# Attention on one core: TensorE's program regrouped, both heads' scores in one tile of three banks, value products' parts added on the way out of PSUM

## The chip, the cores and the metric

The kernel runs on one core of a Trainium2 chip. The metric is the device time of one execution in microseconds, as the median of several runs; less is better.

## What is computed

Two transformer blocks follow each other on 1024 tokens of width 1024, all in fp32. The change lies in the attention of the first. It has two kinds of head, eight each, of width 64: a windowed one (kind a: a block of 128 queries sees its own and the two neighbouring blocks of keys, 256 context keys and a sink) and a neighbourhood one (kind b: 128 queries see up to 384 keys with a bias, and 256 context keys).

```python
s_loc = einsum('bnqkgd,bnjkd->bnkgqj', qb, kb) * scale      # a; masked to the window
s_ctx = einsum('bnqkgd,bjkd->bnkgqj', qb, k_ctx) * scale
p = softmax(concatenate([s_loc, s_ctx, sink_col], axis=-1))
o_a = einsum(p_loc, vb) + einsum(p_ctx, v_ctx)
s_loc = einsum('bnqhd,bnjhd->bnhqj', qb, kg) * scale + bias # b; masked to the neighbourhood
p = softmax(concatenate([s_loc, s_ctx], axis=-1))
o_b = einsum(p_loc, vg) + einsum(p_ctx, v_ctx)
```

## The kernel before, in words

A fp32 factor of most products is cut into an upper part in the format fp32r and a lower part, the rest. The attention works on 64 units (`units`): 32 of kind a (block i, pair of heads p), then 32 of kind b (pair p, block i). A unit is two heads e = 0, 1 of one block of 128 queries, with three tiles of 128 local keys (two for i = 0 and 7) and two of context keys. Per unit these steps follow each other, each in a helper:

- `f_s` (L936): the scores of one head into PSUM, by the query's two parts: two products for the local keys (L948) and two for the context (L949). Each head has a tile `ps_s` of two banks, with two buffers. The order of local and context columns is chosen by `order` (L908) so that no product crosses a bank.
- `f_max` (L952): VectorE adds mask or bias, writes the negated scores to `sp` and reduces them to the softmax's shift (L961). It is the last reader of the score tile.
- `f_exp` (L966): ScalarE's exponential in place, with its sum (L971).
- `f_pt` (L974): the probabilities are transposed by TensorE (L241), four blocks of 128x128 to a bank, in groups 0, 1 and 2, into a PSUM tile `pp` (`pp_tile`, three buffers), and cut into the two parts in `pt`. For group 0 ScalarE copies the bank out (L993) and GpSimd makes both parts (L994, L995); for groups 1 and 2 ScalarE makes the upper part (L997) and VectorE the lower (L998).
- `f_pv` (L1000): the value products into the one bank of `ps_v`. For kind a (L1011) a block's two heads share a product, upper part and lower part in turn, accumulated in PSUM; for kind b (L1016) a product has one head's upper and lower part side by side, and their two results stay apart in PSUM. `part` is the half of the work (a) or the head (b). ScalarE copies the result out (L1022).
- `f_fin` (L1026): fp32 products with `twice` (L1035), a 128x64 matrix of two stacked identities, turn the result round and add what is still apart: one product per head for kind a, two for kind b. VectorE copies it to `O` (L1036).

The loop at L1179 runs software-pipelined: in step n, unit n gets its scores and reductions, unit n-1 the exponentials, unit n-2 the transposes, unit n-3 the value products, unit n-4 `f_fin`. Every second step turns a q tile (`conv_q`, L888, also a `pp` tile), whose reading also lets SP's queue issue the next q loads. Extra work is hung onto fixed steps: stacking kind b's keys (`b_k`: transposes on TensorE, copies on ScalarE, subtractions on VectorE), their values (`b_v`, GpSimd), the bias (`b_bias`: a product at L1106, sums on VectorE), normalizations (GpSimd L1050, L1057, L1069; a VectorE root at step 40, L248 to L261), and pieces of the next stage's weights (L142, L143). Each engine runs its instructions in the order in which this program issues them; a tile's buffer is given out again when all users of its last contents are done. In step n before, TensorE's order is: scores of head 0, group 0, scores of head 1, group 1, value products part 0, group 2, value products part 1, `f_fin`, q tile, extras.

Of the kernel before, what the change touches and what calls it, by code (L numbers as in the profile page):

```python
# [9 lines left out]
F32 = mybir.dt.float32  # L10
R32 = mybir.dt.float32r
I32 = mybir.dt.int32
AF = mybir.ActivationFunctionType
ALU = mybir.AluOpType
# [4 lines left out]
P = 128  # L19
D = 1024  # L20
KD = 8
S = 1024
# [190 lines left out]
def kernel(ctx: ExitStack, tc: tile.TileContext, a: dict, out: bass.AP, dbg=None):  # L213
    nc = tc.nc
# [25 lines left out]
    def tr(o, i, idn):  # L240
        nc.tensor.transpose(o, i, idn)  # L241
# [22 lines left out]
    ident = const.tile([P, P], F32, name="ident")  # L264
# [171 lines left out]
    for i in range(3):  # L436
        pt = ps_t.tile([P, 512], F32, tag="tp", name="vtp", bufs=2)
# [43 lines left out]
    for j in range(4):  # L481
        c = slice(j * 512, j * 512 + 512)
# [9 lines left out]
    for v in range(2):  # L492
        nc.vector.tensor_tensor(out=msum[:, v], in0=pmod[:, :, v], in1=bm, op=ALU.add)
        nc.vector.scalar_tensor_tensor(out=ab[:, v, 0], in0=msum[:, v, 8:16], scalar=1.0,
                                       in1=vec[:, voff["norm1"]:voff["norm1"] + 8], op0=ALU.add, op1=ALU.mult)
# [347 lines left out]
    zeros = zero1.broadcast_to([P, CTX])  # L843
    st_ps = ExitStack()
    ps_s = pool("ps_s", space=PSUM, stack=st_ps)
    ps_p = pool("ps_p", space=PSUM, stack=st_ps)
# [4 lines left out]
    maskA = wk.tile([P, 896], F32, name="maskA")  # L851
    twice = wk.tile([P, 64], F32, name="twice")
# [9 lines left out]
    A = {}  # L862

    def pp_tile():
        return ps_p.tile([P, 512], F32, tag="pp", name="pp", bufs=3)

    def stack_k(src, dst_a, dst_b, cols):

# [12 lines left out]
    def kt(i):  # L881
        return [j for j in (i - 1, i, i + 1) if 0 <= j < 8]
# [22 lines left out]
    def v_stack(u, e, tt):  # L905
        return VA[:, tt, u[2] // 2, :] if u[0] == "a" else B["v", u[2]][:, tt, e, :]

    def order(u, e):  # L908

        kk = kt(u[1])  # L910
        first = u[1] == 7 if u[0] == "a" else 0 < u[1] < 7 and e == 1
        return [8, 9] + kk if first else kk + [8, 9]

    def addends(u, e):

        i, p, nl = u[1], u[2], len(kt(u[1])) * P
        if u[0] == "a":
            a0 = 384 if i == 0 else 0 if i == 7 else 256
            return [(0, nl + 256, maskA[:, a0:a0 + nl + 256])]
        if i in (0, 7):  # L920
            ed = B["bE", p][:, e, (1 if i == 0 else 0):(3 if i == 0 else 2)].rearrange("p s r c -> p (s r c)")
            return [(0, nl, ed), (nl, 256, zeros)]
        return [(0, 640, B["bI", p][:, 0:640] if e == 0 else B["bI", p][:, 384:1024])]

    def stat(u):
# [8 lines left out]
    st = {}  # L934

    def f_s(x, e):  # L936
        u = units[x]
        kk = kt(u[1])
        nl = len(kk) * P
        c1 = order(u, e)[0] == 8  # L940
        w = nl + 256
        a0 = 512 - (256 if c1 else nl)
        ps = ps_s.tile([P, 1024], F32, tag="s", name="ps_s", bufs=2)[:, a0:a0 + w]
        lo, co = (256, 0) if c1 else (0, nl)
        k = k_stack(u, e)
        for z in range(2):
            q = qhl[x // 2][z][:, 2 * (x % 2) + e]
            nc.tensor.matmul(ps[:, lo:lo + nl], q, k[:, kk[0] * P:kk[0] * P + nl], start=(z == 0), stop=(z == 1))  # L948
            nc.tensor.matmul(ps[:, co:co + 256], q, k[:, 1024:1280], start=(z == 0), stop=(z == 1))  # L949
        st["s", x, e] = ps  # L950

    def f_max(x, e):  # L952

        u = units[x]
        if e == 0:
            st["sp", x] = wk.tile([P, 2, 640], F32, tag="sp", name="sp", bufs=3)
            st["nm", x] = stat(u)
        ps, nm = st.pop(("s", x, e)), st["nm", x][0][:, e:e + 1]
        at0 = nsink[:, 2 * u[2] + e:2 * u[2] + e + 1] if u[0] == "a" else -NEG
        for c0, n, in1 in addends(u, e):  # L960
            nc.vector.tensor_tensor_reduce(  # L961
                out=st["sp", x][:, e, c0:c0 + n], in0=ps[:, c0:c0 + n], in1=in1, scale=1.0, scalar=at0,
                op0=ALU.add, op1=ALU.min, accum_out=nm)
            at0 = nm

    def f_exp(x, e):  # L966
        u = units[x]
        nm, sm = st["nm", x]
        sp = st["sp", x]
        w = len(kt(u[1])) * P + 256  # L970
        nc.scalar.activation(out=sp[:, e, :w], in_=sp[:, e, :w], func=AF.Exp, bias=nm[:, e:e + 1], scale=-1.0,  # L971
                             accum_out=sm[:, e:e + 1])

    def f_pt(x, gi):  # L974
        u = units[x]
        nk = len(kt(u[1])) + 2
        if gi == 0:
            st["pt", x] = wk.tile([P, 10, 2, P], R32, tag="pt", name="pt", bufs=2)
        pt = st["pt", x]
        sp = st["sp", x] if gi < 2 else st.pop(("sp", x))  # L980
        g = list(range(4 * gi, min(4 * gi + 4, 2 * nk)))
        if not g:
            return
        pp = pp_tile()
        for x_, b in enumerate(g):
            j, e = b // 2, b % 2
            tr(pp[:, x_ * P:(x_ + 1) * P], sp[:, e, j * P:(j + 1) * P], ident)
        w = len(g) * P
        ph, pl = pt[:, g[0]:g[0] + len(g), 0, :], pt[:, g[0]:g[0] + len(g), 1, :]
        pv = pp[:, :w].rearrange("p (b t) -> p b t", t=P)  # L990
        if gi == 0:
            pf = wk.tile([P, 4, P], F32, tag="pf", name="pf", bufs=2)
            nc.scalar.activation(out=pf, in_=pv, func=AF.Copy)  # L993
            nc.gpsimd.tensor_copy(out=ph, in_=pf)  # L994
            nc.gpsimd.tensor_tensor(out=pl, in0=pf, in1=ph.bitcast(F32), op=ALU.subtract)  # L995
        else:
            nc.scalar.activation(out=ph, in_=pv, func=AF.Copy)  # L997
            nc.vector.tensor_tensor(out=pl, in0=pv, in1=ph.bitcast(F32), op=ALU.subtract)  # L998

    def f_pv(x, part):  # L1000
        u = units[x]
        tiles = [order(u, e) for e in range(2)]
        nt_ = len(tiles[0])
        pt = st["pt", x]
        if part == 0:
            st["po", x] = ps_v.tile([P, 512], F32, tag="pv", name="po")
        po = st["po", x]
        if u[0] == "a":
            for j in (range(nt_ - 2) if part == 0 else range(nt_ - 2, nt_)):
                for z in range(2):  # L1010
                    nc.tensor.matmul(po[:, 0:256], v_stack(u, 0, tiles[0][j]), pt[:, 2 * j:2 * j + 2, z, :],  # L1011
                                     start=(j == 0 and z == 0), stop=(j == nt_ - 1 and z == 1))
        else:
            e = part
            for j, tt in enumerate(tiles[e]):
                nc.tensor.matmul(po[:, e * 256:e * 256 + 256], v_stack(u, e, tt),  # L1016
                                 pt[:, 2 * j + e].rearrange("p z t -> p (z t)"),
                                 start=(j == 0), stop=(j == nt_ - 1))
        if part == 1:
            w = 256 if u[0] == "a" else 512  # L1020
            oT = wk.tile([P, 512], F32, tag="oT", name="oT", bufs=2)
            nc.scalar.activation(out=oT[:, :w], in_=po[:, :w], func=AF.Copy)  # L1022
            st["oT", x] = oT
            del st["pt", x], st["po", x]

    def f_fin(x):  # L1026

        kind, i, p = units[x]
        oT = st.pop(("oT", x))
        nb = 1 if kind == "a" else 2  # L1030
        po = pp_tile()
        for e in range(2):
            for j in range(nb):
                b = (nb * e + j) * P
                nc.tensor.matmul(po[:, e * 64:e * 64 + 64], oT[:, b:b + P], twice, start=(j == 0), stop=(j == nb - 1))  # L1035
        nc.vector.tensor_copy(out=O[0 if kind == "a" else 1][:, i, p * 128:p * 128 + 128], in_=po[:, 0:128])  # L1036


# [122 lines left out]
    for t in (maskB.rearrange("p r c -> p (r c)"), maskR, jrev):  # L1161
# [7 lines left out]
                            in0=maskP.rearrange("p (b c s) -> p b s c", s=8, c=8),  # L1169
# [6 lines left out]
    def ok(x):  # L1176
        return 0 <= x < NU

    for n in range(NU + 5):  # L1179
        if n == 35:  # L1180
            switch_pools()
        if ok(n):
            f_s(n, 0)
            f_max(n, 0)
        if ok(n - 1):
            f_exp(n - 1, 0)
        if ok(n - 2):
            f_pt(n - 2, 0)
        if ok(n):
            f_s(n, 1)  # L1190
            f_max(n, 1)
        if ok(n - 1):
            f_exp(n - 1, 1)
        if ok(n - 2):
            f_pt(n - 2, 1)
        if ok(n - 3):
            f_pv(n - 3, 0)
        if ok(n - 2):
            f_pt(n - 2, 2)
        if ok(n - 3):  # L1200
            f_pv(n - 3, 1)
        if ok(n - 4):
            f_fin(n - 4)
        if n % 2 == 0:
            conv_q(n // 2 + 1)
        for f, args in extra.get(n, []):
            f(*args)
# [242 lines left out]
    for i in range(8):  # L1450
        nc.gpsimd.tensor_tensor(out=O[1][:, i], in0=O[1][:, i],
                                in1=oss[:, 24 + i:25 + i].broadcast_to([P, 512]), op=ALU.mult)
    early = {}
    for n4 in range(2):
# [8 lines left out]
        for t in range(8):  # L1463
            ps = early.pop(t, None)
# [780 lines left out]
```

## Time and profile before

| | us |
|---|---|
| median of three runs | 2670.6 (2665.9 to 2671.87) |
| the profiled execution | 2668.49 |
| its span, from first to last instruction | 2666.7 |
| of it, TensorE busy | 2576.5 |
| VectorE, ScalarE, GpSimd busy | 1645.7, 1058.8, 1148.6 |

The attention's first score product starts at 312.73 us of the span, and its last product ends at about 624. The seven stretches below begin at the first score product of steps 0, 6, 18, 29, 36, 47 and 60. In the rows below PE is TensorE's product unit, PEld its weight loads, DVE is VectorE, ACT is ScalarE, POOL is GpSimd and SP is SyncE. A line such as L961 is one of the kernel's source lines; many rows of the trace stand on a helper's line, so tiles tell more than lines. The end of a TensorE row is modelled, and the rows of a stream overlap: their cost is the distance from start to start.

### The profile page before, as it was taken

The page shows a single profiled execution, that of the slowest core. Times are in us where ns is not written, and L with a number is a line of the kernel's source. Part 1 is how long each engine was busy: PE and PEld are TensorE (multiplying, and loading weights), DVE is VectorE, ACT ScalarE, POOL GpSimd, SP SyncE. Part 2 cuts the span into 40 slices and gives each one's busy share as a digit, 9 for nine tenths or more (in the row PEclk, how much of TensorE's full clock was granted, in tenths as well). Part 3 has the DMA queues.
Part 4 walks back from the last instruction along what each step waited for, and adds up shares of the span by engine and source line. Part 5 has one row for each costly group of instructions (what it writes and reads, how often), then busy time and mean ns, then how long its engine had stood idle before and what let it go on. Part 6 is the DMA issues. An engine that isn't in the chain of part 4 may idle for free. (4 is left out here: it accounts for less than half of the span.)

```text
span 2666.7 us, 37138 instructions
## 1 busy us (share of the span) xinstructions
PE 2576.5 (97%) x14053; PEld 2154.0 (81%) x14053; DVE 1645.7 (62%) x3003; ACT 1058.8 (40%) x2613; POOL 1148.6 (43%) x1071
## 2 busy tenths in 40 slices
PE   7999999999989999999999999999999999999998
PEld 3999898899977888888878877877777777777786
DVE  3688678774565555555556432422777777777776
ACT  4644488785232222222223534322433333333333
POOL 2355355564446666666653221212333333333321
PEclk9999999999999999999999999999999999999999
DMA  6166522212111111111111111110111111111112
GB/s 245 33 192 200 147 56 54 73 49 88 33 40 48 48 52 59 48 48 55 56 48 41 50 48 32 32 48 32 49 39 48 48 48 48 48 48 48 48 48 87
DMA packets 152540, 170.87 MB, mean 64 GB/s; under 512 B 39444, under 2 KB 135460, under 8 KB 151336
## 3 DMA queue, kind: packets, MB, share of 16 engines
q1 hardware_dynamic: 152200, 168.35, 19.9%
q8 instruction: 111, 1.82, 0.3%
q0 software_dynamic: 160, 0.14, 0.1%
q14 instruction: 69, 0.57, 0.1%
HBM read 154.81 MB, written 13.65 MB: 63 GB/s over the span
## 5 line engine op out<-in xcount | busy, mean ns | idle before, releaser
L140 POOL TENSOR_TENSOR wlo<-raw,whi 128x512 fp32r<-128x512 f32 x132 | 176.7, 1343 | 476.7 <-ACT whi L139 447.8
L1697 PE MATMUL pgu<-h,whi 128*128 128x512 f32 x864 | 342.4, 396 | 3.1 <-DVE h L1633 3.1
L1698 PE MATMUL pgu<-h,wlo 128*128 128x512 f32 x864 | 341.2, 395 | 0.5 <-POOL wlo L140 0.5
L1696 PE MATMUL pgu<-h,whi 128*128 128x512 f32 x864 | 341.4, 395 | 0.0
L140 DVE TENSOR_TENSOR wlo<-raw,whi 128x512 fp32r<-128x512 f32 (+2 forms) x304 | 221.3, 741 | 149.5 <-ACT whi L139 148.9
L139 ACT ACTIVATE whi<-raw 128x512 fp32r<-128x512 f32 (+1 forms) x436 | 232.2, 552 | 151.1 <-DMA raw<-in_w_down 61.0
L1715 DVE TENSOR_TENSOR uv<-pgu,uv 128x512 f32<-128x512 f32 x216 | 147.7, 687 | 150.0 <-PE pgu L1698 128.6
L237 PE MATMUL pdn<-wlo,hid 128*128 128x512 f32 x576 | 227.3, 395 | 4.5 <-DVE wlo L140 4.5
L236 PE MATMUL pdn<-whi,hid 128*128 128x512 f32 x576 | 226.4, 393 | 1.3 <-DVE uv L1410 1.0
L238 PE MATMUL pdn<-whi,hid 128*128 128x512 f32 x576 | 226.6, 393 | 0.0
L1411 POOL TENSOR_TENSOR x<-x,uv 128x512 f32<-128x512 f32 x144 | 192.2, 1355 | 31.6 <-DVE uv L1410 28.7
L1697 PEld LDWEIGHTS pgu<-h,whi 128*128 128x128 f32 x864 | 162.3, 188 | 42.3 <-DVE h L1633 3.6
L1696 PEld LDWEIGHTS pgu<-h,whi 128*128 128x128 f32 x864 | 162.5, 188 | 40.1
L1698 PEld LDWEIGHTS pgu<-h,wlo 128*128 128x128 f32 x864 | 162.1, 188 | 39.9 <-POOL wlo L140 0.9
L1718 POOL TENSOR_TENSOR uv<-uv 128x512 f32<-128x512 f32 x72 | 109.7, 1524 | 169.1 <-DVE uv L1715 169.1
L1566 POOL TENSOR_TENSOR hid<-sg,hid 128x512 fp32r<-128x512 f32 x80 | 118.0, 1479 | 132.0 <-ACT hid L1565 129.9
L236 PE MATMUL pin<-whi,h 128*128 128x256 f32 x512 | 146.8, 287 | 6.1 <-ACT hsq L634 2.5
L237 PE MATMUL pin<-wlo,h 128*128 128x256 f32 x512 | 146.7, 286 | 1.7 <-DVE wlo L140 1.7
L238 PE MATMUL pin<-whi,h 128*128 128x256 f32 x512 | 146.5, 286 | 0.0
L237 PEld LDWEIGHTS pdn<-wlo,hid 128*128 128x128 f32 x576 | 108.1, 188 | 34.1 <-DVE wlo L140 9.6
L236 PEld LDWEIGHTS pdn<-whi,hid 128*128 128x128 f32 x576 | 108.2, 188 | 27.8 <-DVE uv L1410 1.5
L1407 DVE TENSOR_TENSOR x<-pdn,x 128x512 f32<-128x512 f32 x160 | 105.3, 685 | 38.8 <-PE pdn L238 29.0
(391 smaller groups left out, 6951.0 us busy)
## 6 DMA issues: line engine op xcount, KB each, us to landing
raw<-in_ffn_w_up SPq DMA_DIRECT2D x22, 1024.0 KB
mraw<-in_w_mod SPq DMA_DIRECT2D x32, 512.0 KB
raw<-in_w_gate SPq DMA_DIRECT2D x11, 1024.0 KB
raw<-in_w_up SPq DMA_DIRECT2D x11, 1024.0 KB
raw<-in_w_down SPq DMA_DIRECT2D x11, 1024.0 KB
raw<-in_ffn_w_down SPq DMA_DIRECT2D x11, 1024.0 KB
raw<-in_w_in SPq DMA_DIRECT2D x9, 1024.0 KB
wm<-in_w_mod SPq DMA_DIRECT2D x8, 1024.0 KB
```

Of the source, the lines that this page charges most:

```text
L139: nc.scalar.activation(out=hi, in_=src, func=AF.Copy)
L140: (engine or self.engine or nc.vector).tensor_tensor(out=lo, in0=src, in1=hi.bitcast(F32), op=ALU.subtract)
L236: nc.tensor.matmul(ps, lh, rh, start=(i == 0), stop=False)
L237: nc.tensor.matmul(ps, lh, rl, start=False, stop=False)
L238: nc.tensor.matmul(ps, ll, rh, start=False, stop=(i == n - 1))
L1411: nc.gpsimd.tensor_tensor(out=xs, in0=xs, in1=tmp, op=ALU.add)
L1566: nc.gpsimd.tensor_tensor(out=hl[:, c], in0=sg[:, cc, c], in1=hh[:, c].bitcast(F32), op=ALU.subtract)
L1696: nc.tensor.matmul(ps, lh, rh, start=start and k == 0, stop=False)
L1697: nc.tensor.matmul(ps, lh, rl, start=False, stop=False)
L1698: nc.tensor.matmul(ps, ll, rh, start=False, stop=stop and k == n - 1)
L1715: nc.vector.tensor_tensor(out=o, in0=ps, in1=u, op=ALU.add)
L1718: nc.gpsimd.tensor_tensor(out=o, in0=u, in1=v, op=ALU.add)
```

## The change

- In a step TensorE now has both heads' scores, then both parts of the value products, then all groups of transposes, then `f_fin`.
- Both heads' scores of a unit lie in one tile of three banks with one buffer: head 0's local keys end at the first bank's end, the context columns of both heads share the second, head 1's local keys begin the third. So head 0 has its columns as local, context and head 1 as context, local. `order` goes; `place` finds a block's columns, and a mask that doesn't fit one reduction is applied in two (kind a, i = 0 for head 1 and i = 7 for head 0).
- `pp` has four buffers in place of three.
- For kind b the two parts of the value products are added by VectorE while they leave PSUM, so that `f_fin` has one product per head there too.

```diff
     def pp_tile():
-        return ps_p.tile([P, 512], F32, tag="pp", name="pp", bufs=3)
+        return ps_p.tile([P, 512], F32, tag="pp", name="pp", bufs=4)
...
-        c1 = order(u, e)[0] == 8
-        w = nl + 256
-        a0 = 512 - (256 if c1 else nl)
-        ps = ps_s.tile([P, 1024], F32, tag="s", name="ps_s", bufs=2)[:, a0:a0 + w]
-        lo, co = (256, 0) if c1 else (0, nl)
+        if e == 0:
+            st["S", x] = ps_s.tile([P, 1536], F32, tag="s", name="ps_s", bufs=1)
+        ps = st["S", x] if e == 0 else st.pop(("S", x))
+        lo, co = (1024, 768) if e else (512 - nl, 512)
...
         if part == 1:
-            w = 256 if u[0] == "a" else 512
             oT = wk.tile([P, 512], F32, tag="oT", name="oT", bufs=2)
-            nc.scalar.activation(out=oT[:, :w], in_=po[:, :w], func=AF.Copy)
+            if u[0] == "a":
+                nc.scalar.activation(out=oT[:, :256], in_=po[:, :256], func=AF.Copy)
+            else:
+                pz = po.rearrange("p (e z t) -> p z e t", e=2, z=2)
+                hi = oT[:, 256:512].rearrange("p (e t) -> p e t", e=2)
+                nc.scalar.activation(out=hi, in_=pz[:, 0], func=AF.Copy)
+                nc.vector.tensor_tensor(out=oT[:, :256].rearrange("p (e t) -> p e t", e=2), in0=pz[:, 1], in1=hi,
+                                        op=ALU.add)
...
-            for j in range(nb):
-                b = (nb * e + j) * P
-                nc.tensor.matmul(po[:, e * 64:e * 64 + 64], oT[:, b:b + P], twice, start=(j == 0), stop=(j == nb - 1))
+            nc.tensor.matmul(po[:, e * 64:e * 64 + 64], oT[:, e * P:(e + 1) * P], twice, start=True, stop=True)
...
         if ok(n):
-            f_s(n, 0)
-            f_max(n, 0)
+            for e in range(2):
+                f_s(n, e)
+            for e in range(2):
+                f_max(n, e)
         if ok(n - 1):
-            f_exp(n - 1, 0)
+            for e in range(2):
+                f_exp(n - 1, e)
+        if ok(n - 3):
+            for e in range(2):
+                f_pv(n - 3, e)
         if ok(n - 2):
-            f_pt(n - 2, 0)
-        if ok(n):
-            f_s(n, 1)
-            f_max(n, 1)
-        if ok(n - 1):
-            f_exp(n - 1, 1)
-        if ok(n - 2):
-            f_pt(n - 2, 1)
-        if ok(n - 3):
-            f_pv(n - 3, 0)
-        if ok(n - 2):
-            f_pt(n - 2, 2)
-        if ok(n - 3):
-            f_pv(n - 3, 1)
+            for g in range(3):
+                f_pt(n - 2, g)
```

## Rows read from the trace of the kernel before

**Rows 1.** The page's first line: span and number of instructions.

```profile
span 2666.7 us, 37138 instructions
```

**Rows 2.** Windows view: stretch, length, busy us (instructions) of PE, PEld, DVE, ACT, POOL; granted clock.

```profile
312.73:335.51 22.78, 18.36 (x124) 17.49 (x125) 15.99 (x36) 15.82 (x37) 10.93 (x13) 0.78 0.31 77
335.51:387.18 51.67, 50.73 (x408) 49.38 (x408) 38.95 (x98) 45.12 (x111) 25.74 (x28) 1.00 0.16 36
387.18:442.99 55.81, 50.50 (x392) 47.27 (x392) 48.96 (x117) 46.95 (x113) 31.00 (x37) 1.00 0.22 53
442.99:469.75 26.76, 26.07 (x221) 25.48 (x220) 21.19 (x60) 25.15 (x64) 14.51 (x15) 1.00 0.46 122
469.75:533.68 63.93, 57.88 (x440) 54.48 (x440) 47.91 (x133) 48.22 (x106) 38.23 (x50) 0.97 0.25 61
533.68:595.76 62.08, 60.27 (x492) 58.32 (x491) 47.51 (x135) 50.82 (x114) 38.23 (x45) 1.00 0.21 52
595.76:625.93 30.17, 28.09 (x236) 27.40 (x235) 18.35 (x63) 24.82 (x60) 15.24 (x21) 1.00 0.03 11
```

**Rows 3.** Timeline of TensorE, most of one quiet step: start, length, row, number merged.

```profile
358.10 0.60 PE L241 MATMUL pp<-ident,sp 128*128 128x128 f32 x4
...
358.83 0.34 PE L948 MATMUL ps_s<-kstA,q 128*128 128x384 f32 x1
359.01 0.28 PE L949 MATMUL ps_s<-kstA,q 128*128 128x256 f32 x1
359.13 0.60 PE L241 MATMUL pp<-ident,sp 128*128 128x128 f32 x4
359.49 0.95 PE L1011 MATMUL po<-pt,VA 128*128 128x256 f32 x6
360.28 0.38 PE L241 MATMUL pp<-ident,sp 128*128 128x128 f32 x2
360.42 0.72 PE L1011 MATMUL po<-pt,VA 128*128 128x256 f32 x4
360.97 0.56 PE L1035 MATMUL pp<-twice,oT 128*128 128x64 f32 x4
361.34 0.42 PE L948 MATMUL ps_s<-kstA,q 128*128 128x384 f32 x1
```

**Rows 4.** Timelines of TensorE, ScalarE and GpSimd: one unit's group 0 in the next step.

```profile
362.01 0.60 PE L241 MATMUL pp<-ident,sp 128*128 128x128 f32 x4
...
362.73 0.60 ACT L993 ACTIVATE pf<-pp 128x512 f32<-128x512 f32 x1 [0.30 <-PE pp L241]
...
363.39 0.61 POOL L994 CAST pt<-pf 128x512 fp32r<-128x512 f32 x1
364.09 1.28 POOL L995 TENSOR_TENSOR pt<-pf,pt 128x512 fp32r<-128x512 f32 x1
```

**Rows 5.** Timeline of TensorE at the attention's end: the last unit's value products.

```profile
620.92 1.21 PE L1016 MATMUL po<-pt,vB 128*128 128x256 f32 x8 [0.29 <-POOL pt L995]
621.97 0.45 PE L1035 MATMUL pp<-twice,oT 128*128 128x64 f32 x3
```

**Rows 6.** Groups of instructions, TensorE, 312 to 625 us: `f_fin`'s rows.

```profile
L1035 PE MATMUL pp<-twice,oT 128*128 128x64 f32 x384 | 49.8, 266 | 0.0
```

**Rows 7.** View of TensorE's waits, 320 to 624 us: total us, times, longest.

```profile
PE pp L241 <- DVE pt L998: 10.6, 21, 1.1
...
PE ps_s L948 <- DVE bstat L961: 1.6, 1, 1.6
...
PE pp L1106 <- DMA braw<-in_rpbz: 1.0, 1, 1.0
```

**Rows 8.** Groups of instructions, VectorE, 312 to 625 us: busy, mean ns, idle before.

```profile
L961 DVE CUSTOM_DVE_ANT_0 sp<-ps_s,maskA,nsink 128x640 f32<-128x640 f32 x48 | 40.4, 875 | 0.5
...
L998 DVE TENSOR_TENSOR pt<-pp,pt 128x256 fp32r<-128x256 f32 x48 | 19.9, 414 | 0.0
```

**Rows 9.** Timeline of VectorE in step 24: a weight piece ahead of a reduction.

```profile
419.87 1.34 DVE L143 SCALAR_TENSOR_TENSOR wlo<-raw,vec,whi 128x256 fp32r<-128x256 f32 x1
```

More of the change, by code (lines that the diff above doesn't have):

```diff
@@ L906, in v_stack, with tiles_of, place @@
         return VA[:, tt, u[2] // 2, :] if u[0] == "a" else B["v", u[2]][:, tt, e, :]
[L908 to L912, printed above, removed]
+    def tiles_of(u):
+        return kt(u[1]) + [8, 9]
+    def place(u, e, j):
+        nl = len(kt(u[1]))
+        return j if e == 0 else (j + 2 if j < nl else j - nl)
     def addends(u, e):
         i, p, nl = u[1], u[2], len(kt(u[1])) * P
+        lo, co = (256, 0) if e else (0, nl)
         if u[0] == "a":
-            a0 = 384 if i == 0 else 0 if i == 7 else 256
-            return [(0, nl + 256, maskA[:, a0:a0 + nl + 256])]
+            m0 = 384 if i == 0 else 256
+            if (i, e) in ((0, 1), (7, 0)):
+                return [(lo, nl, maskA[:, m0:m0 + nl]), (co, 256, zeros)]
+            m0 -= lo
+            return [(0, nl + 256, maskA[:, m0:m0 + nl + 256])]
         if i in (0, 7):
             ed = B["bE", p][:, e, (1 if i == 0 else 0):(3 if i == 0 else 2)].rearrange("p s r c -> p (s r c)")
-            return [(0, nl, ed), (nl, 256, zeros)]
+            return [(lo, nl, ed), (co, 256, zeros)]
         return [(0, 640, B["bI", p][:, 0:640] if e == 0 else B["bI", p][:, 384:1024])]
@@ L949, in f_s @@
             nc.tensor.matmul(ps[:, co:co + 256], q, k[:, 1024:1280], start=(z == 0), stop=(z == 1))
-        st["s", x, e] = ps
+        st["s", x, e] = ps[:, min(lo, co):min(lo, co) + nl + 256]
     def f_max(x, e):
@@ L986, in f_pt @@
             j, e = b // 2, b % 2
-            tr(pp[:, x_ * P:(x_ + 1) * P], sp[:, e, j * P:(j + 1) * P], ident)
+            c = place(u, e, j) * P
+            tr(pp[:, x_ * P:(x_ + 1) * P], sp[:, e, c:c + P], ident)
         w = len(g) * P
@@ L1001, in f_pv @@
         u = units[x]
-        tiles = [order(u, e) for e in range(2)]
-        nt_ = len(tiles[0])
+        tiles = tiles_of(u)
+        nt_ = len(tiles)
         pt = st["pt", x]
@@ L1010, in f_pv @@
                 for z in range(2):
-                    nc.tensor.matmul(po[:, 0:256], v_stack(u, 0, tiles[0][j]), pt[:, 2 * j:2 * j + 2, z, :],
+                    nc.tensor.matmul(po[:, 0:256], v_stack(u, 0, tiles[j]), pt[:, 2 * j:2 * j + 2, z, :],
                                      start=(j == 0 and z == 0), stop=(j == nt_ - 1 and z == 1))
@@ L1014, in f_pv @@
             e = part
-            for j, tt in enumerate(tiles[e]):
+            for j, tt in enumerate(tiles):
                 nc.tensor.matmul(po[:, e * 256:e * 256 + 256], v_stack(u, e, tt),
@@ L1029, in f_fin @@
         oT = st.pop(("oT", x))
-        nb = 1 if kind == "a" else 2
         po = pp_tile()
         for e in range(2):
-            for j in range(nb):
-                b = (nb * e + j) * P
-                nc.tensor.matmul(po[:, e * 64:e * 64 + 64], oT[:, b:b + P], twice, start=(j == 0), stop=(j == nb - 1))
+            nc.tensor.matmul(po[:, e * 64:e * 64 + 64], oT[:, e * P:(e + 1) * P], twice, start=True, stop=True)
         nc.vector.tensor_copy(out=O[0 if kind == "a" else 1][:, i, p * 128:p * 128 + 128], in_=po[:, 0:128])
```

## The prediction

> **What bounds the kernel now.** I read the page first, for the span: 2666.7 us [rows 1], in an execution of 2668.5 us. The change touches only the attention, so I then cut that stage into stretches along its steps [rows 2]. In all seven TensorE is the busiest engine: 50.73 of 51.67 us in steps 6 to 17, 50.50 of 55.81 in steps 18 to 28, 57.88 of 63.93 in steps 36 to 46. So the stage is TensorE's own work plus waits, and both have to be priced. The timeline of one quiet step [rows 3] gives the work. From one step's first transposes to the next step's, 358.10 to 362.01 [rows 4], it takes 3.91 us. A transpose is 0.11 us (four rows 0.60, two rows 0.38, so 0.22 for two), a value product 0.117 (six rows 0.95, four rows 0.72), a pair of score products 0.30 (358.83 to 359.13). Eight score products are 1.20, ten transposes 1.09, ten value products 1.17, and f_fin's four rows 0.45 (0.37 from 360.97 to 361.34; a product that follows a row of the other kind starts 0.08 early and lasts that much longer). The sum is 3.91. Every second step also turns a q tile, four transposes for 0.44, 4.35 in all. A step without waits already runs at TensorE's floor.
>
> The waits come from the view of waits [rows 7]: TensorE waited 10.6 us, 21 times, for VectorE's L998, the release of one of the three pp tiles. Single waits of 1.6 us (for a reduction that stood behind L260 and its neighbours on VectorE) and 1.0 us (for a bias row's DMA, which SP issues behind q loads; the change moves neither) come on top.
>
> **The change part by part.**
>
> *f_fin.* The 384 rows of L1035 [rows 6] are two for each fp32 product: 128 for the 32 units of kind a, 256 for kind b. The change leaves two products instead of four in a b unit, so 128 rows go; at 0.111 us each that is 14.2 us of TensorE's time, 0.44 a step. In exchange VectorE gets one addition of 128x256 out of PSUM in each b unit, nearest to the 0.414 us of L998's smaller form; the ends are nothing and a reduction's 0.875 [rows 8]. ScalarE copies half the columns. VectorE is busy 47.5 of 62.1 us in steps 47 to 59 [rows 2], so 13 times 0.41 fits beside TensorE; uncovered it would cost 0.41 x 32 = 13 us.
>
> *Fourth pp tile.* The 10.6 us of rows 7 should go: with four tiles and three transposing groups in a row, group 0 takes the tile that group 1 or f_fin had a step earlier, and that is long read.
>
> *Grouping.* Here I looked for a price of going between fp32r products and fp32 transposes. In rows 3, two transposes at 360.28 stand between value products. From there to f_fin at 360.97, two transposes and four products take 0.69 us, and 2 x 0.109 + 4 x 0.117 is 0.69. The whole step has eight alternations and fits its floor to the 0.02 us that the rows' rounding leaves. Six alternations fewer gain at most 0.02 a step, 1.3 us in 64. The Trainium skill's TensorEngine Tiling (Array Packing), Key Properties, says that going from one tiling mode to another drains TensorE. It is said of tilings and not of number formats, and no such drain shows between these two kinds of row; what it would give is among the rivals.
>
> *Value products against the lower parts.* This is the new wait, and I take it to decide. Group 0's transposes are copied out by ScalarE (L993), and GpSimd makes both parts of them (L994, L995). Rows 4 show the chain with ScalarE free: transposes from 362.01, copy at 362.73, cast at 363.39, subtraction from 364.09 to 365.37. That is 3.36 us from the first transpose; 0.06 us lie between the copy's end and the cast, and I add 0.04 (an estimate) for the signal to TensorE. So value products can't run sooner than 3.40 us after their unit's first transpose. Before, they come 359.49 + 3.91 - 358.10 = 5.30 us after it [rows 3]: hidden. After, TensorE's program between them is ten transposes, f_fin, the q tile if it is due, and eight score products: 1.09 + 0.45 + 1.20 = 2.74 us, or 3.18 with a q tile. So it waits 0.66 or 0.22 us, in every step. Behind the waiting product on TensorE are all other value products, the next unit's transposes (which start the same chain again) and f_fin, so this closes a loop: 3.40 plus the value products. After such a wait eight products take 621.97 - 620.92 = 1.05 us [rows 5]. Kind a waits at its second product (the first needs the upper part alone), so 1.05 + 0.12 = 1.17 follow; kind b has ten, 1.28. A step takes 4.57 (a) or 4.68 (b), and 4.33 or 4.45 for the eight units of each kind with two key tiles. The floor holds only where TensorE's rows between are longer than 3.40: b steps with stacked keys (4.87) or a bias product of 0.84 us (4.84 without and 5.27 with a q tile).
>
> *One score tile.* The second head's context product and the first head's lie in one bank, so the first reduction can't start until all eight products are through, 0.6 us later; and TensorE may write unit n+1's scores only when both of unit n's reductions (0.88 us each [rows 8], 0.81 from start to start) are done. Where it doesn't wait for GpSimd, scores end some 1.2 us before the step's first transpose, so the reductions end about 0.7 us behind that transpose; the next scores are due 1.5 us behind it. With L143's 1.34 us ahead of them on VectorE [rows 9] they end at about 2.3, and the scores are 0.8 us late, of which the 0.66 us spent waiting for GpSimd covers most. I take nothing. The Trainium skill's PSUM — Partial Sum Buffer, PSUM bank collisions, speaks against this layout: TensorE writing and VectorE reading one bank at a time is an error there, even in other columns. Here that only adds the 0.6 us just told, which is hidden; no run shows the collision itself. The two units that now need a split reduction (4 pairs of each) add about 0.2 us on VectorE, covered too.
>
> *Sum, stretch by stretch* (before from [rows 2]), from score start to score start. Steps 0 to 5: 22.78 before; unit 1's scores wait for two reductions in place of one (+0.9), unit 2's again, and three units of two key tiles take 4.33 in place of about 3.8: +4, and +1 because TensorE stands at a granted 0.78 in this stretch and will be kept low longer. Steps 6 to 17: 4.33 + 11 x 4.57 = 54.6, +2.9. Steps 18 to 28: 11 x 4.57 = 50.3, 1.6 for two steps with stacked keys and two with a bias product, an allowance of 1.3 for ScalarE's key copies ahead of group 0, 0.4 for a q tile at the end: 53.6, -2.2. Steps 29 to 35: two at 4.57, four at 4.33, one at 4.45, less 0.2: 30.7, +3.9. Steps 36 to 46: five at 4.68, two at 4.87, 5.27, 4.84 and two at 4.45, 52.2 by the rule, and 1.1 for what stands ahead of the last scores; the 1.0 and 1.6 us of rows 7 stay; 2 is an allowance for GpSimd's normalizations and ScalarE's key copies queued ahead of group 0: 57.9, -6.0. Steps 47 to 59: two at 5.27, five at 4.68, 4.87, 4.84, four at 4.45, an allowance of 1.1 for ScalarE and GpSimd, and 1.3 less ahead of the first scores: 61.3, -0.8. From 595.76 to the last value product's end, 622.13 [rows 5], were 26.4 us; six loops of 4.68, the last unit's 3.40 + 1.05, less the 1.54 by which scores lead, are 31.0, +4.6, and the addition joins the last chain, +0.4. In all 4 + 1 + 2.9 - 2.2 + 3.9 - 6.0 - 0.8 + 4.6 + 0.4 = +7.8; I round to +7. On the profiled execution that is 2675.5 us. It lies 2.1 us under the median of the three runs, 2670.6; on that, 2677.6, so 2678. What the change saves in crowded steps it pays back in quiet ones.
>
> **The rivals.**
>
> *The savings stay (faster).* One mechanism: GpSimd's two operations end before TensorE comes to the value products, because TensorE is itself longer busy between, or is held up evenly by something else. It decides where 2.74 us of rows exceed 3.40. For it: in steps with stacked keys or a bias they do. Against it: the sum of rows 4, with no row in the chain that the change shortens. Then f_fin's 14.2 and the pp waits' 10.6 come off: 2670.6 - 25 = 2646; with half of the steps covered some 2658.
>
> *The score tile is the loop (slower).* VectorE, not GpSimd, sets the step: if both reductions end more than 2.2 us behind the first transpose (1.5 until scores are due, 0.66 of cover), the rest is lost. It takes 0.8 us of other VectorE work than now lies ahead of them. For it: 20 or so steps with L143, bias sums or stacked keys, and the waits of rows 7 that fall there now. At 0.8 us in 20 steps more: +16, 2694.
>
> *The clock falls (slower).* TensorE would wait in most steps. Rows 2 show what waits did so far: granted 1.00, that is 2.4 GHz, in steps 18 to 28 although TensorE was idle in 5.3 of 55.8 us, and 0.78 in the first stretch, with 4.4 of 22.8 us idle, and 0.97 around the wait of 1.6. Waits of 0.7 us are below that. At 1.2 GHz the 3.9 us of a step would be 7.8, over 200 us in all. The Trainium skill's TensorE: Matmul & The Clock Gate, Part 4: PE-mode transpose, says that transposes don't count as busy time in the way products do, which would make ten in a row and a wait the worse; by it this rival would hold, but a third of the quiet step is transposes already, at 1.00.
>
> *Alternation was the cost (faster).* If each of the six alternations cost a drain of 0.16 us (six value products last 0.95, and 0.95 - 5 x 0.117 - 0.08 = 0.28 is one, 0.16 more than its 0.117), 61 us would go: 2610. The floor's fit in rows 3 is against it.
>
> **How the numbers follow.** The forecast, the loop of 3.40 us, has a chance of 0.56; the savings stay 0.20; the score tile 0.17; the clock 0.03; alternation 0.02; in the last 0.02 nothing changes. About 0.2% (5.3 us) is what a measurement of this kernel can tell from no change. Half of a tenth of a microsecond in the loop is 3 us in 60 steps, the ends of ScalarE's and VectorE's terms are worth 5 either way, so the forecast's own range is 2668 to 2688. Its chance splits into 0.31 slower, 0.23 same, 0.02 faster; of the savings 0.15 are faster and 0.05 within; of the score tile 0.13 slower and 0.04 same; clock 0.03 slower; alternation 0.02 faster; the last 0.02 same. That gives 0.47 slower, 0.34 same, 0.19 faster. The range reaches to half covered steps below and to most of the score tile's case above: 2656 to 2692.
>
> **What would show it.** In the profile after: L1035 with 256 rows in place of 384; no wait for L998 at pp; waits of TensorE at L1011 and L1016 for POOL L995, 0.2 to 0.7 us in some 50 steps; quiet steps at 4.5 to 4.7 us with and without a q tile alike; steps 36 to 46 about 6 us shorter and steps 6 to 17 about 3 longer. Waits at L948 for L961 in most steps would mean the score tile; neither of the two, that the chain is shorter than I added it. A floor of less than 3.85 us in a step without waits would mean that alternations cost something.

## The result

The changed kernel takes 2684.5 us (median of four runs, 2683.27 to 2685.57) against 2670.7 before: a ratio of 1.0055, with a 95% interval of 1.0038 to 1.0072. It is slower, by 13.8 us; the prediction had 2678.0, some 7 us slower, in a range of 2656 to 2692. The profiled execution took 2683.86 us.

The page's first line, then the windows view of the seven stretches, cut at the first score products of the same steps as [rows 2]; the last one ends at the start of the last row of the turning (`f_fin`), which before came at 623.71.

```profile
span 2682.1 us, 36934 instructions
313.69:341.56 27.87, 19.85 (x124) 18.21 (x125) 17.41 (x44) 16.72 (x38) 9.90 (x11) 0.76 0.22 54
341.56:396.15 54.59, 51.84 (x409) 49.41 (x408) 39.57 (x98) 45.40 (x112) 26.05 (x28) 1.00 0.15 36
396.15:453.33 57.18, 50.64 (x393) 47.15 (x392) 45.13 (x116) 46.88 (x112) 30.10 (x37) 1.00 0.21 50
453.33:483.79 30.46, 27.11 (x221) 25.60 (x220) 24.31 (x67) 25.81 (x64) 14.07 (x16) 1.00 0.45 117
483.79:544.08 60.29, 53.25 (x397) 48.86 (x396) 51.65 (x146) 47.61 (x109) 38.55 (x50) 0.97 0.24 60
544.08:605.68 61.60, 56.06 (x441) 52.05 (x439) 50.24 (x147) 47.27 (x111) 37.77 (x47) 1.00 0.21 52
605.68:639.79 34.11, 27.30 (x195) 25.71 (x195) 19.08 (x59) 23.52 (x59) 16.78 (x22) 0.91 0.01 1
```

Against [rows 2], TensorE's busy time falls from 57.88 to 53.25 us in steps 36 to 46, yet the stretch is only 3.6 us shorter. In steps 6 to 17 nothing was added to TensorE's program, and 2.9 us are lost. The view of TensorE's waits, 300 to 645 us (total us, times, longest), names what it stands still for:

```profile
PE po L1024 <- POOL pt L1003: 11.5, 18, 1.9
PE po L1019 <- POOL pt L1003: 8.7, 18, 0.9
PE ps_s L955 <- DVE stat L968: 7.3, 5, 3.8
PE pp L241 <- DVE pt L1006: 3.7, 6, 0.8
PE pp L1117 <- DVE pt L1006: 2.7, 5, 0.6
PE ps_s L955 <- DVE bstat L968: 2.4, 2, 2.2
```

L1019 and L1024 are the value products of kinds a and b, L1003 is GpSimd's subtraction, L955 a score product, L968 the reduction, L1006 VectorE's lower part, L1117 the bias product. The new wait is the one that the prediction named as deciding: 36 waits for GpSimd, 20.2 us. But the wait for the lower part at pp, 10.6 us in [rows 7], has not gone: 11 waits, 6.4 us.

Two quiet steps of kind a (steps without extra work; the first turns a q tile), in the timelines of TensorE, ScalarE and GpSimd:

```profile
370.09 0.28 PE L1019 MATMUL po<-pt,VA 128*128 128x256 f32 x1
370.79 1.31 PE L1019 MATMUL po<-pt,VA 128*128 128x256 f32 x9 [0.42 <-POOL pt L1003]
371.94 1.25 PE L241 MATMUL pp<-ident,sp 128*128 128x128 f32 x10
...
372.66 0.60 ACT L1001 ACTIVATE pf<-pp 128x512 f32<-128x512 f32 x1
...
373.32 0.61 POOL L1002 CAST pt<-pf 128x512 fp32r<-128x512 f32 x1 [1.58 <-ACT pf L1001]
374.01 1.30 POOL L1003 TENSOR_TENSOR pt<-pf,pt 128x512 fp32r<-128x512 f32 x1
...
375.06 1.62 PE L1019 MATMUL po<-pt,VA 128*128 128x256 f32 x10
376.52 1.25 PE L241 MATMUL pp<-ident,sp 128*128 128x128 f32 x10
```

From the transposes at 371.94 GpSimd's subtraction is done at 375.31, 3.37 us later; the next transposes come at 376.52, after 4.58 us. The prediction's loop is 4.57. In the first of the two steps the second value product waits openly (0.42 us). In the second the wait hides: ten value products last from 375.06 to 376.52, 1.46 us where 10 x 0.117 is 1.17, and no gap is marked, as the first product's modelled end covers nearly all of it.

### The profile page after: what moved, and what is told of

The parts are those of the page before. It is cut to its first block, busy times and chain, and to the rows that moved or that the text cites. A ratio compares the mean times of both kernels' runs of the same rounds, so it can differ in the third digit from the quotient of the medians.

```text
span 2682.1 us, 36934 instructions
## 1 busy us (share of the span) xinstructions
PE 2571.2 (96%) x13925; PEld 2141.1 (80%) x13925; DVE 1654.1 (62%) x3051; ACT 1056.1 (39%) x2613; POOL 1145.9 (43%) x1071
```

## The experiments

Three theories were to be told apart: the *loop* (value products wait for GpSimd's part of their own unit), the *score tile* (VectorE's reductions set the step), and the price of going between products and transposes (a change of kind). Besides these the value of `f_fin`'s rows and of the fourth pp tile were to be measured. Line numbers in the rows of e1, e3, e4, e5, e7 and e9 are those of after, or within a few lines of them; in e2 and e6 they are near those of before.

Beside the experiments the kernel before took 2666.5 to 2667.1 us, where it took 2670.7 beside the change, and the four runs of e1 lie 8 us apart. Each ratio goes by the kernel before that was measured beside it; a few us between two experiments are not told by their medians. The attention in the traces, one execution each, leaves the other stages out. From the first score product to the last row of the turning it lasts, in us:

| before | after | e1 | e2 | e3 | e4 | e5 | e6 | e7 | e8 | e9 |
|---|---|---|---|---|---|---|---|---|---|---|
| 311.0 | 326.1 | 291.0 | 304.2 | 326.7 | 312.2 | 350.4 | 299.5 | 286.6 | 295.3 | 332.1 |

### e1_pt_first: all transposes ahead of the value products

```diff
+        if ok(n - 2):
+            for g in range(3):
+                f_pt(n - 2, g)
         if ok(n - 3):
             for e in range(2):
                 f_pv(n - 3, e)
-        if ok(n - 2):
-            for g in range(3):
-                f_pt(n - 2, g)
```

> The changed kernel with one move: in a step all transposes of unit n-2 come before the value products of unit n-3, and not behind them. Nothing is added or removed. The value products then have a whole step between them and their own unit's transposes (some 5 us in place of 2.7), while the distance between a unit's reductions and the next unit's scores stays what it is. Loop theory (the value products wait for GpSimd's lower part): the 36 waits of TensorE for it, 20.2 us and about 0.16 us more for each resumption, so 26 us, go; the time is 2655 to 2663, faster than the kernel before, and quiet steps without a q tile come to 3.9 us and with one to 4.35. Score-tile rival (VectorE's reductions set the step): the waits move to the score products, and the time stays at 2680 or more.

Measured: 2648.7 us (2644.61 to 2653.02), ratio to the kernel before 0.9928 (0.9908 to 0.9948). The waits view, then the timeline of a step with its q tile:

```profile
PE ps_s L955 <- DVE stat L968: 7.1, 5, 3.3
PE ps_s L955 <- DVE bstat L968: 3.5, 2, 3.0
...
PE pp L241 <- DVE pt L1006: 2.9, 6, 0.9
...
PE po L1024 <- POOL pt L1003: 0.7, 1, 0.7
```

```profile
372.49 1.25 PE L241 MATMUL pp<-ident,sp 128*128 128x128 f32 x10
373.50 1.42 PE L1019 MATMUL po<-pt,VA 128*128 128x256 f32 x10
...
376.75 1.25 PE L241 MATMUL pp<-ident,sp 128*128 128x128 f32 x10
```

One wait of 36 is left, that of the very last unit, and the step is 4.26 us with its q tile (3.87 without). The score-tile rival falls as the cause of the slowdown: the waits at L955 for reductions are still there (10.6 us, 9.7 in after), and the time has fallen all the same. The gain is 36 us (35.1 in the attention) where I had counted 26 from the list of waits; the time lies 6 us below the range that I gave it. Three things that I had left out are in the rest: work that waited without a listed gap (some 0.3 us in each step of kind a without a q tile, as in the second step above), waits at pp for L1006, 7 of 3.5 us here in place of 11 of 6.4, and a granted clock of 0.91 in the last stretch of after, 1.00 here.

### e2_fin_only: the addition leaving PSUM, in the kernel before

```diff
-            nc.scalar.activation(out=oT[:, :w], in_=po[:, :w], func=AF.Copy)
...
+                nc.scalar.activation(out=hi, in_=pz[:, 0], func=AF.Copy)
+                nc.vector.tensor_tensor(out=oT[:, :256].rearrange("p (e t) -> p e t", e=2), in0=pz[:, 1], in1=hi,
+                                        op=ALU.add)
...
-            for j in range(nb):
-                b = (nb * e + j) * P
-                nc.tensor.matmul(po[:, e * 64:e * 64 + 64], oT[:, b:b + P], twice, start=(j == 0), stop=(j == nb - 1))
+            nc.tensor.matmul(po[:, e * 64:e * 64 + 64], oT[:, e * P:(e + 1) * P], twice, start=True, stop=True)
```

> The kernel before with one part of the change alone: VectorE adds the two parts of kind b's value products as they leave PSUM, and the turning has one product per head. 128 rows of 0.111 us leave TensorE, 14.2 us in all. If TensorE's own work sets the time in kind b's steps and VectorE's addition is hidden, the time is 2656 to 2660. If VectorE's additions, in front of its other work, lengthen the waits for a transposing group's tile, part of it is lost: 2662 to 2670. Were GpSimd's chain already a loop in the kernel before, nothing is gained: 2669 to 2672.

Measured: 2661.9 us (2661.15 to 2664.59), ratio 0.9986 (0.9976 to 0.9995): 4.9 us of the 14.2 (6.8 in the attention). The waits say where the others went:

```profile
PE pp L241 <- DVE pt L998: 14.0, 23, 1.4
```

10.6 us became 14.0. In step 44, for instance, the step's own rows are 0.45 us less and the step is 6.25 us before and after: TensorE comes 0.45 us earlier to a tile that VectorE releases when it did before.

### e3_old_fin: the change without it

```diff
+        nb = 1 if kind == "a" else 2
         po = pp_tile()
         for e in range(2):
-            nc.tensor.matmul(po[:, e * 64:e * 64 + 64], oT[:, e * P:(e + 1) * P], twice, start=True, stop=True)
+            for j in range(nb):
+                b = (nb * e + j) * P
+                nc.tensor.matmul(po[:, e * 64:e * 64 + 64], oT[:, b:b + P], twice, start=(j == 0), stop=(j == nb - 1))
```

(and ScalarE's copy of the whole bank in place of copy and addition)

> The changed kernel with that part undone: f_fin has its two products per head for kind b again, and ScalarE copies the whole bank. Loop theory: in kind b's quiet steps the four rows more (0.44 us) lie between the transposes and the value products, where TensorE waits anyway, so they cost nothing there; they cost 0.44 us only in the 10 to 14 crowded steps of kind b (stacked keys, bias products, q tiles), so the time is 2684 to 2691. If the 14.2 us were won in the changed kernel, and something else lost them, the time is 2697 to 2700.

Measured: 2684.0 us (2681.9 to 2684.64), ratio 1.0063 (1.0048 to 1.0078); with the change it was 1.0055 (1.0038 to 1.0072), so the two can't be told apart. The value products of step 48, in the timeline of e3 and then of after:

```profile
550.52 1.42 PE L1024 MATMUL po<-pt,vB 128*128 128x256 f32 x10 [0.37 <-POOL pt L1003]
```

```profile
549.98 1.42 PE L1024 MATMUL po<-pt,vB 128*128 128x256 f32 x10 [0.78 <-POOL pt L1003]
```

The 0.44 us that `f_fin` no longer takes come back as 0.41 us of waiting. In this order the 128 rows are worth next to nothing: 0.6 us of the attention. Up to step 60 after is 2.2 us ahead, of which the last stretch takes 1.6 back: there its granted clock is 0.91, and e3's is 1.00.

### e4_g0_no_pool: group 0 without GpSimd

```diff
-        if gi == 0:
+        if False:
             pf = wk.tile([P, 4, P], F32, tag="pf", name="pf", bufs=2)
```

> The changed kernel with group 0 treated as groups 1 and 2 are: ScalarE makes the upper part and VectorE the lower one straight from PSUM, and GpSimd has no part in it. The chain from a unit's first transpose to its last lower part then lacks GpSimd's cast and subtraction (0.7 and 1.3 us). VectorE gets 64 subtractions more, of some 0.7 us. Loop theory: TensorE's waits for GpSimd's lower part go, and what is left is what VectorE's queue adds: with 39 of 52 us busy in steps 6 to 17 and 8 us more, it still fits, so 2660 to 2675. Score-tile rival: VectorE is what sets the step, and each step becomes longer by up to 0.7 us: 2700 to 2730, with waits of the score products for the reductions.

Measured: 2669.6 us (2667.21 to 2676.77), ratio 1.001 (1.000 to 1.0019), 15 us less than after though VectorE has 64 subtractions more. No wait for GpSimd is left; VectorE, now with all three groups, releases the pp tiles too late instead:

```profile
PE pp L241 <- DVE pt L1006: 17.1, 27, 1.7
PE ps_s L955 <- DVE stat L968: 7.5, 7, 3.3
```

So with another producer, too, the waits at the value products go with GpSimd's chain (three are left at the attention's end, 1.4 us, for VectorE's part); and the reductions, though VectorE is fuller, still don't set the step.

### e5_three_pp: three pp tiles in the changed order

```diff
-        return ps_p.tile([P, 512], F32, tag="pp", name="pp", bufs=4)
+        return ps_p.tile([P, 512], F32, tag="pp", name="pp", bufs=3)
```

> The changed kernel with three pp tiles again in place of four; all else stays. The q tile of every second step then takes the tile of group 1 of the same step, which VectorE's lower part releases some 2.4 us after the first transpose, while TensorE comes to it 1.5 us after it. If the fourth tile is what keeps that wait away, q tiles wait some 0.9 us in about 30 steps; the wait for GpSimd's lower part that follows shrinks by as much as it was there (0.35 to 0.6), so 0.3 to 0.5 us a step is left, and the time is 2690 to 2702. If the fourth tile does nothing (the prediction's 10.6 us of waits went for another reason), it stays at 2683 to 2687.

Measured: 2709.5 us (2708.47 to 2712.11), ratio 1.0156 (1.014 to 1.0171), 25 us above after and over 7 above what I gave it at most.

```profile
PE pp L241 <- DVE pt L1006: 17.9, 28, 0.9
PE pp L1046 <- ACT pf L1001: 7.5, 14, 1.2
```

The q tiles wait as expected; that `f_fin`, fourth in the row, then waits for group 0's copy I had left out. The three groups one behind another make the fourth tile necessary; it isn't a bonus beside the new order.

### e6_two_tiles: e1's order on the kernel before's PSUM layout

```diff
 (e2_fin_only, with its loop as in e1_pt_first)
             for e in range(2):
                 f_s(n, e)
                 f_max(n, e)
...
             for g in range(3):
                 f_pt(n - 2, g)
...
             for e in range(2):
                 f_pv(n - 3, e)
```

> The order of e1_pt_first (scores, all transposes, value products, turning) with the kernel before's PSUM layout: two score tiles of two banks, one for each head, and three pp tiles; the parts are added leaving PSUM as in the change. Against e1_pt_first it undoes the one score tile and the fourth pp tile. If the one score tile is what makes e1_pt_first's score products wait (12 us of waits for reductions and key stacks, most of them in the first steps and around steps 21, 23, 32 and 41), these shrink by 5 to 9 us, and with the value products between a step's transposes and its q tile three pp tiles are enough: 2640 to 2646. If three pp tiles are too few, waits for VectorE's lower part come at transposes and bias products in the crowded steps, and the time is 2650 to 2662. Going between fp32r products and transposes is free if a quiet step without a q tile takes the same 3.89 to 3.92 us as in e2_fin_only, where products and transposes take turns; if changes of kind cost something, it is shorter here by 0.03 us or more.

Measured: 2657.8 us (2656.82 to 2660.22), ratio 0.9963 (0.995 to 0.9976): 9 us more than e1.

```profile
PE pp L241 <- DVE pt L998: 6.4, 14, 0.6
PE pp L241 <- DVE kstB L878: 6.1, 8, 0.8
PE ps_s L948 <- DVE stat L961: 2.8, 1, 2.8
PE ps_s L948 <- DVE bstat L961: 2.1, 1, 2.1
```

Two score tiles do take 5.7 us off the score products' waits for reductions (7.1 + 3.5 to 2.8 + 2.1), but the missing fourth pp tile costs more. In this order the bank won by the single score tile is worth more as a pp tile. And the quiet steps of kind a without a q tile and without a wait take 3.87 or 3.88 us in e1, 3.88 here (steps 7, 11 and 15; the others, 9, 13 and 17, take 4.21 here) and 3.89 to 3.92 in e2: four changes of kind fewer (four a step in place of eight) are worth 0.01 to 0.05 us a step, close to what the rows can tell.

### e7_extras_early: e1 with the extras' pp tiles ahead of the value products

```diff
+        for f, args in extra.get(n, []):
+            if f in (b_k, b_bias):
+                f(*args)
         if ok(n - 3):
             for e in range(2):
                 f_pv(n - 3, e)
...
         for f, args in extra.get(n, []):
-            f(*args)
+            if f not in (b_k, b_bias):
+                f(*args)
```

> e1_pt_first with the transposes of kind b's keys and the bias products moved within their step: right behind the unit's transposes, ahead of the value products, and no longer behind the q tile. They then take the pp tile of the step before and no longer that of group 1 of the same step, and by the q tile's turn group 1's tile has been read. If the sixth tile of a step is what brings the waits at pp for VectorE's lower part (7 in e1_pt_first, 3.5 us and some 0.16 us more for each resumption), they go, and the time is 2642 to 2646. If these waits come from VectorE's queue whatever tile is asked for, they move to another row and the time stays at 2647 to 2651.

Measured: 2643.4 us (2642.63 to 2648.99), ratio 0.9912 (0.9895 to 0.9929), the best of all here: 23.6 us below the kernel before and 41 below the change.

```profile
PE ps_s L955 <- DVE stat L968: 5.5, 3, 3.4
PE ps_s L955 <- DVE bstat L968: 3.4, 2, 2.8
...
PE pp L241 <- DVE pt L1006: 0.7, 2, 0.5
```

The waits at pp for L1006 shrink from 3.5 to 0.7 us, by the place of two kinds of extra work alone; the attention is 4.4 us shorter than in e1.

### e8_early_old_fin: e7 with the old turning

The edit is that of e3.

> e7_extras_early with the turning of the kernel before: two products per head for kind b, no addition on VectorE. It prices the 128 rows of f_fin a third time, where TensorE runs nearly without waits. If they are worth their 14.2 us wherever TensorE sets the time, the time is 2655 to 2659 against 2643.4 without them. If half is lost in crowded steps, as in e2_fin_only (5 of 14.2 us gained), it is 2647 to 2652.

Measured: 2651.6 us (2650.85 to 2656.02), ratio 0.9944 (0.9928 to 0.9961): 8.1 us more than e7 (8.7 in the attention). The same 128 rows are worth next to nothing in after, some 5 us in the kernel before and 8 us here, of 14.2 that they last.

### e9_extras_ahead: the sixth tile, in the change's own order

```diff
         if ok(n - 3):
             for e in range(2):
                 f_pv(n - 3, e)
+        for f, args in extra.get(n, []):
+            if f in (b_k, b_bias):
+                f(*args)
         if ok(n - 2):
             for g in range(3):
                 f_pt(n - 2, g)
```

> The changed kernel, its order kept, with the transposes of kind b's keys and the bias products moved ahead of the unit's transposes (behind the value products) and no longer last in the step. The q tile then takes group 0's tile, which ScalarE has read early, and no transpose or product takes the tile that group 1 filled in the same step. If the sixth pp tile of a step is what left waits for VectorE's lower part in the changed kernel (11 at L241 and L1117, 6.4 us), these go. The time gains less: where such a step also turns a q tile, the loop from transposes to value products (4.57 us) and 0.44 us of key transposes ahead of it make 5.0 in place of 5.5, some 5 us in eleven steps; but the moved rows no longer lie between transposes and value products, so in the seven or so steps without a q tile, where they covered GpSimd's chain, 0.3 to 0.66 us of waits for it come back, some 3 us. So 2680 to 2684, with waits for GpSimd's lower part grown from 20.2 to 24 us or more. If VectorE's queue and not the choice of tile makes those waits, they stay at pp, under other tiles.

Measured: 2689.8 us (2687.31 to 2693.35), ratio 1.0086 (1.007 to 1.0103), 5 us above after (6.0 in the attention) and 6 above the range that I gave it. The waits at pp behave as expected, the time doesn't. No wait for L1006 at a pp tile is left, and the waits for GpSimd have grown to 22.6 us, less than the 24 I gave them; but a wait has come that I had not seen:

```profile
PE po L1024 <- POOL pt L1003: 12.4, 20, 1.9
PE po L1019 <- POOL pt L1003: 10.2, 20, 1.0
PE pp L1046 <- ACT pf L1001: 7.8, 10, 1.0
```

```profile
407.98 0.59 ACT L874 ACTIVATE kstB<-pp 64x512 fp32r<-64x512 f32 x1
408.58 0.59 ACT L875 ACTIVATE kstB<-pp 64x512 fp32r<-64x512 f32 x1
409.19 0.60 ACT L1001 ACTIVATE pf<-pp 128x512 f32<-128x512 f32 x1
```

In ScalarE's timeline of step 20 the two key copies stand ahead of group 0's copy: the head of GpSimd's chain is 1.2 us later, and `f_fin` waits 0.81 us for the tile that this copy releases. Moving work on TensorE moved it on ScalarE too, and there it stood ahead of the loop.

## Why the prediction came out as it did

The direction, the likeliest case and the range held; the size was about half of what was measured. In us, change against before, from first score product to first score product (the last row to the last row of the turning):

| | before | predicted | after | e1 | e7 |
|---|---|---|---|---|---|
| ahead of step 0 | 312.73 | 0 | +1.0 | +0.1 | +0.2 |
| steps 0 to 5 | 22.78 | +5 | +5.1 | +3.3 | +3.5 |
| steps 6 to 17 | 51.67 | +2.9 | +2.9 | -3.1 | -3.1 |
| steps 18 to 28 | 55.81 | -2.2 | +1.4 | -5.6 | -7.2 |
| steps 29 to 35 | 26.76 | +3.9 | +3.7 | -0.3 | -0.3 |
| steps 36 to 46 | 63.93 | -6.0 | -3.6 | -5.0 | -8.7 |
| steps 47 to 59 | 62.08 | -0.8 | -0.5 | -7.2 | -6.5 |
| step 60 to the end | 27.95 | +5.0 | +6.2 | -2.1 | -2.1 |

The after column sums to 16.1; 0.7 come back by the next stage's first product, and the profiled executions differ by 15.4.

*Value products against the lower parts* held, in mechanism and in size: 3.40 us predicted from transposes to released value products, 4.57 for the step, 4.58 measured, and the two stretches of quiet steps that it rules (6 to 17, 29 to 35) within 0.2 us. Steps 0 to 5 fit too, but of their 5.1 us 3.3 stay in e1 without the loop; they go with the reductions that the scores wait for there and with the low clock, as the sum had it. e1 and e4 take the loop away by two different edits, and its waits go in both. What I had wrong is only how it looks: I expected 0.2 to 0.7 us in some 50 steps; the list has 36 waits, since in steps without a q tile the loss often hides inside the value products. Steps alternate between 4.96 and 4.18 instead of all being alike, because I counted from transposes and the step is cut at its scores; their mean is 4.57.

*Fourth pp tile* is the step that failed. "The 10.6 us of rows 7 should go" was argued from group 0 alone, which comes to a tile used a step earlier. It overlooked the sixth tile: an even step with stacked keys or a bias product has three groups, `f_fin`, the q tile and the extra's tile, and the extra must take one that VectorE's L1006 of the same step has not yet read. The timelines of TensorE and VectorE in step 20 of after:

```profile
410.53 0.61 PE L241 MATMUL pp<-ident,qraw 128*128 128x128 f32 x4
411.70 0.66 PE L241 MATMUL pp<-ident,kr 128*128 128x128 f32 x4 [0.56 <-DVE pt L1006]
...
410.95 1.02 DVE L1006 TENSOR_TENSOR pt<-pp,pt 128x512 fp32r<-128x512 f32 x2 [0.88 <-ACT pt L1005]
```

The key transposes could start at 410.53 + 4 x 0.109 = 410.97, and start 0.73 us later. Of that the list shows 0.56, since it counts from the modelled end of the q tile's row, 410.53 + 0.61 = 411.14. All 11 such waits lie in the even steps 18 to 26, 36, 38, 44, 46, 52 and 54; steps 42 and 50, which have a q tile and keys but a unit of two groups only, need five tiles and show none. With 0.16 us more for each the waits cost 3.5 us in steps 18 to 28, as much as that stretch's error; 3.0 in steps 36 to 46, where the error is 2.4; and 1.6 in steps 47 to 59, where by luck my allowances covered it. That the errors come from these waits alone is worked out, not shown: other terms were off as well (two waits for reductions, 1.4 us, which the sum put at nothing, lie in steps 18 to 28 too). That the sixth tile makes the waits is shown: e9 takes them away in the change's own order, where others come in their place and no time is gained, and e7 does so in e1's, where it gains some 5 us.

*f_fin* was right as a count (L1046 has 256 rows), and the sum by steps did not count it as a gain where the loop rules; e3 shows that it is next to none. But "14.2 us of TensorE's time" and the rival in which "f_fin's 14.2" come off took the rows at their full length. Where TensorE next waits for a tile on VectorE's schedule they are worth less: 5 us in e2, 8 in e8.

*Grouping* cost and gained next to nothing, as the fit of [rows 3] said: 0.01 to 0.05 us a step for four of the six changes of kind, where I had 0.02 as the most for all. The 61 us of the alternation rival are excluded.

*One score tile* was rightly taken as hidden in quiet steps. It shows at the start (waits at L955 up to 3.8 us, inside the +5 given there), 0.67 and 0.70 us at the ends of steps 21 and 23, and 2.2 us at the end of step 41 in place of the 1.6 of [rows 7]. No run shows what happens when two engines touch one bank at a time.

*The clock* took more than the 1.2 us that the last stretch lost beyond its +5.0; the sum had a term for the clock in the first stretch alone. In the windows view of after, two stretches at the attention's end stand at a granted 0.50, that is 1.2 GHz, each from 0.5 us behind the end of a wait for GpSimd:

```profile
626.66:630.07 3.41, 3.41 (x18) 3.41 (x18) 0.42 (x1) 1.23 (x5) 0.27 (x1) 0.50 0.00 0
636.90:643.70 6.80, 6.55 (x31) 5.75 (x29) 2.93 (x16) 3.10 (x9) 2.13 (x4) 0.50 0.36 82
```

```profile
626.15 2.11 PE L1024 MATMUL po<-pt,vB 128*128 128x256 f32 x10 [1.67 <-POOL pt L1003]
628.05 2.24 PE L241 MATMUL pp<-ident,sp 128*128 128x128 f32 x10
...
631.82 1.45 PE L1024 MATMUL po<-pt,vB 128*128 128x256 f32 x10 [1.13 <-POOL pt L1003]
...
636.41 1.70 PE L1024 MATMUL po<-pt,vB 128*128 128x256 f32 x8 [1.87 <-POOL pt L1003]
637.91 0.95 PE L1046 MATMUL pp<-twice,oT 128*128 128x64 f32 x4
639.10 1.11 PE L1046 MATMUL pp<-twice,oT 128*128 128x64 f32 x4 [0.24 <-DVE oT L1035]
```

In the first of them ten transposes last 2.24 us where they last 1.25 in the steps above, and the next value products come 631.82 - 626.15 = 5.67 us later, where the loop has 4.68: 1.0 us. In the second the last eight value products take 637.91 - 636.41 = 1.50 us against 1.05 in [rows 5], and the last turning rows 0.23 us each (639.10 to 639.79 for three) against 0.11: some 0.8 us. In e3 the last stretch stands at 1.00 throughout, and it is 4.6 us longer than before, not 6.2. In steps 6 to 35, with a wait in nearly every other step and ten transposes in a row, the granted clock stays 1.00. By the sentence of the Trainium skill that the prediction weighed (TensorE: Matmul & The Clock Gate, Part 4: PE-mode transpose) it could have fallen there; the measured 1.00 says that it did not.

The 1.0 us ahead of step 0 lies in the stages before the attention, in code that the change doesn't touch; in the other runs it was between -1.1 and +1.0, so it is the scatter of single executions.

## What to carry to other kernels

Before regrouping an engine's program, measure for each pair of producer and consumer the chain over the other engines against the rows that lie between them: here 3.4 us of chain found 5.3 us of cover in the old order, 2.7 in the new one, and 5 again when only two blocks changed places (e1, 36 us). Count a step's tiles at its fullest, extras included, against the buffers, and ask for each tile which engine releases it. Rows taken off the busiest engine can be worth less than their length where a wait on another engine's schedule comes next: the same 14.2 us were worth next to nothing, 5 and 8.

## What the runs showed of the hardware, unexpected

- The list of waits is a lower bound of waiting. A product held up behind one whose modelled end is later shows no gap: ten value products of 1.17 us took 1.46 with nothing marked.
- A listed wait is counted from the modelled end of the row before, which lies some 0.16 us behind the point where the next row could have started: 0.73 us were lost for a gap of 0.56 in step 20.
- The length of a wait alone did not tell whether the granted clock fell. It stood at 0.50 behind waits of 1.67 and 1.87 us at the attention's end in after; behind waits of 1.33, 1.32 and 1.54 us there in e3 it stayed at 1.00, and so it did in e9 behind two of 1.66 us. In steps 36 to 46 it was 0.97 in before, with a wait of 1.6 us, and 1.00 in e2, with one of 2.0.
